# The order of the first sixteen weight chunks in a one-core hybrid decoder layer

## The chip, the core and the metric
The kernel runs on one core of a Trainium2 chip. The metric is the device time of one execution in microseconds (us). Before the change it is 1804.32 us, the median of three runs (1804.09 to 1804.88).

## The reference, cut to what matters
One decoder layer for 256 tokens of width 2048, in float32: a normed mixer with two parallel branches (mLSTM and RWKV-7), cross-attention into 256 memory tokens, and a gated feed-forward of width 8192. The change concerns its beginning:

```python
h = rms_norm(x, mix_pre_norm[l])          # x: 256 x 2048
proj = h @ w_in                           # 2048 x 10536
mlstm_p, rwkv_p, gate_p = split_cols(proj, (MLSTM_TOTAL, RWKV_TOTAL, GATE_TOTAL))
q, k, v, o, ir, fr = split_cols(mlstm_p, MLSTM_COLS)       # ir, fr: 4 columns each
r, kr, vr, wl, al, gl = split_cols(rp, RWKV_COLS)          # wl, al, gl: 64 + 64 + 160
```

The narrow outputs `ir`, `fr`, `wl`, `al`, `gl` together are 296 columns; `r` is 1024 columns wide. Everything after these projections is the same before and after the change.

## The kernel before, in words
A float32 product is built of three products of rounded numbers: each weight chunk and each tile of x is split into a high part (a rounded copy) and a low part (what the rounding left), and TensorE computes high x high, low x high and high x low. So for each chunk of weights ScalarE makes `wh` (L437) and VectorE makes `wl` (L463), and for each tile of x ScalarE makes the high part with the norm's gain in it and VectorE the low part (L68 is the helper through which these go; L191 is the one through which all matmuls go).

The work is a list of *blocks* (L1501 and on). A block has a list of weight chunks, a function that gives the tiles of x, and an evacuation that reads the sums. Block 0 holds the 296 narrow columns in 8 chunks `op`, each of which carries two k-tiles of x as well (552 KB: 128 partitions, 2 k-tiles, 256 + 296 columns). Block 1 holds 512 columns of `r` in 8 chunks of two k-tiles (`raw`, 512 KB). A chunk of block 1 needs the tiles of x that came with the narrow chunk of the same number.

`Feed` holds the order of chunks and runs ahead of the matmuls by numbers: `dma(n)` issues loads up to chunk n, `hi(n)` makes high parts, `lo(n)` low parts. While chunk i is multiplied, low parts are made up to i + 3 and loads are issued up to i + 7. There are four buffers for `raw` and five each for `wh` and `wl`. All loads but the first few are issued on SP's queue; ScalarE's queue takes three in the beginning (L405, L407, L412). The engines work in the order in which the program hands out instructions; there is no planner at run time.

The order before: `LEAD = 5` narrow chunks, then the other three in turn with the first chunks of block 1 (narrow 5, wide 0, narrow 6, wide 1, narrow 7), then wide 2 to 7 (L393, L594 to L602). The first two narrow chunks are treated apart (`first`, L441): piece by piece, chunk 0 on VectorE and ScalarE, chunk 1's high part on POOL. The wide chunk at place 6 is split in two pieces, so that its first k-tile is ready earlier (`pieces`, L427). `x_piece` (L624) splits the two k-tiles of x of one narrow chunk, and `pre_sm` and `pre_r0` say at which chunk that is done, and at which the squares of x are summed for the norm's statistics (`st0.add`).

Side work (evacuations and all that follows them) is cut into pieces by generators; `Spread.half` runs the next piece at each half of a chunk (each k-tile) if ScalarE and VectorE are thought to have room. The evacuation of block 0 is one such task (`sm_evac`, L672): it ends the statistics (`fold`, then a column of sums on TensorE, `var` on VectorE, a power on POOL, the matmuls `stb` on TensorE), scales the narrow outputs and transposes them. Before a new block starts, the evacuation of the block before the last must be through (`side.need`). Block 0's comes after its eighth chunk.

Of the kernel before, what the change touches and what calls it, by code (L numbers as in the profile page):

```python
# [22 lines left out]
DECAY = -math.exp(-0.5)  # L23
DFF = 8192
NSM = 296
LEAD = 5


_COLS = [
# [9 lines left out]
NPAR = _o  # L39
# [115 lines left out]
def _layer(ctx, tc, nc, d, dbg):  # L155
    act, dve = Meter(nc.scalar, 200.0, 0.83), Meter(nc.vector, 130.0, 1.04)
    pool, pe, sp = nc.gpsimd, nc.tensor, nc.sync
# [7 lines left out]
    def U(name, shape=None, dt=F32):  # L165
        return mp.tile(shape or [P, 8, S], dt, tag="U", bufs=7, name=name)

    def T2(name, shape=None, dt=F32):
        return mp.tile(shape or [P, 2, S], dt, tag="T2", bufs=6, name=name)

    def big(name, shape=None, dt=F32):
        return mp.tile(shape or [P, KD, S], dt, tag="big", bufs=2, name=name)
# [5 lines left out]
    def C(name, tag, shape=None, dt=F32):  # L178
        return mp.tile(shape or [P, S], dt, tag=tag, bufs=1, name=name)
# [7 lines left out]
    def aux(name, shape=None):  # L187
        return pp.tile(shape or [P, 512], F32, tag="aux", bufs=4, name=name)
# [4 lines left out]
    def keep_warm(n):  # L193

        q = aux("warm", [P, P])
        for _ in range(n):
            mm(q, ones.broadcast_to((P, P)), ones.broadcast_to((P, P)))


    par = cp.tile([P, NPAR], F32, name="par")  # L200
# [3 lines left out]
    def pcol(n, i=0, w=1):  # L204
        return par[:, PC[n] + i:PC[n] + i + w]
# [33 lines left out]
    def split(hi, lo, src):  # L239
        act.copy(hi, src)  # L240
        dve.tensor_sub(lo, src, hi)

    def split_gain(hi, lo, src, g):
        act.activation(hi, src, AF.Identity, scale=g)
        dve.scalar_tensor_tensor(lo, src, g, hi, op0=ALU.mult, op1=ALU.subtract)
# [37 lines left out]
    class Stat:  # L283


        def __init__(self, name, tag="ysb1", sq="au", home=None):
            self.name, self.tag, self.sq, self.home = name, tag, sq, home
            self.rc = cp.tile([P, 2], F32, name=name + "_c")
            self.n = 0
            self.done = False  # L290
# [99 lines left out]
    class Feed:  # L390
        def __init__(self):
            a, g = blocks[0]["srcs"], blocks[1]["srcs"]
            self.src = a[:LEAD] + [c for p in zip(a[LEAD:], g) for c in p] + g[len(a) - LEAD:]  # L393
            self.src += [s for b in blocks[2:] for s in b["srcs"]]
            self.raw, self.st, self.nd, self.ns, self.nl, self.nop = {}, {}, 0, 0, 0, 0

        def dma(self, upto):
            while self.nd <= min(upto, len(self.src) - 1):
                s = self.src[self.nd]
                if s.shape[-1] == NSM:  # L400
                    c = self.nop
                    self.nop += 1
                    r = op[c][:, :, S:]
                    if c == 0:
                        act.dma_start(ws0, d["w_s0"])  # L405
                        act.activation(mhalf[:, 0:1], mhalf[:, 0:1], AF.Copy)
                        act.dma_start(r[:, 1], s[:, 1])  # L407
                        for j in range(2):
                            sp.dma_start(xq[0][:, j], d["op"][0, :, j, 0:S])
                    elif c == 1:  # L410
                        sp.dma_start(op[1][:, 0], d["op"][1, :, 0])
                        act.dma_start(op[1][:, 1], d["op"][1, :, 1])  # L412
                    else:
                        sp.dma_start(op[c], d["op"][c])
                else:
                    r = wp.tile(list(s.shape), F32, tag="raw", bufs=4, name="raw")
                    sp.dma_start(r, s)
                self.raw[self.nd] = r
                self.nd += 1

# [5 lines left out]

        def pieces(self, n, *v):  # L427

            return [[t[:, k] for t in v] for k in range(2)] if n == LEAD + 1 else [v]

        def hi(self, upto):
            while self.ns <= min(upto, len(self.src) - 1):
                self.dma(self.ns)
                r = self.raw[self.ns]
                wh = self.staged("wh", r)
                for o, v in self.pieces(self.ns, wh, r):
                    nc.scalar.copy(o, v)  # L437
                self.st[self.ns] = [wh, None]
                self.ns += 1

        def first(self, c):  # L441

            r, wh, wl = self.raw.pop(c), self.staged("wh", self.src[c]), self.staged("wl", self.src[c])
            r = [ws0[:, 16:] if c == kj == 0 else r[:, kj] for kj in range(2)]
            if c == 0:
                nc.vector.tensor_copy(wh[:, 0], r[0])
            for kj in range(2):
                x_split(c, kj)
                if c:
                    pool.tensor_copy(wh[:, kj], r[kj])  # L450
                elif kj:
                    nc.scalar.copy(wh[:, kj], r[kj])
                nc.vector.tensor_sub(wl[:, kj], r[kj], wh[:, kj])
            self.st[c] = [wh, wl]
            self.ns = self.nl = c + 1

        def lo(self, upto):
            self.hi(upto)
# [15 lines left out]

    def run():
        feed = Feed()
        for c in range(8):
            x_load(c)
            feed.dma(c if c < LEAD else min(c * 2 - LEAD + 1, 10))
        i = 0  # L480
        pend = []

# [111 lines left out]
        side.ahead = lambda: feed.hi(feed.ns)  # L594
        side.ahead_lo = lambda: feed.lo(feed.nl)
        one, two = work(blocks[0]), work(blocks[1])
        for _ in range(LEAD):
            next(one)
        for _ in one:
            next(two)  # L600
        for _ in two:
            pass  # L602
        for b in blocks[2:]:
# [10 lines left out]
    op = [big("op0", [P, 3, 2, NX]), big("op1", [P, 3, 2, NX])]  # L614
    op = [op[c // 3][:, c % 3] for c in range(6)] + [U(f"op{c}", [P, 2, NX]) for c in (6, 7)]
    xq = [o[:, :, 0:S] for o in op]
    ws0 = C("ws0", "bg1", [P, 16 + NSM])
    xs0 = lambda k: (hh[:, k], hl[:, k])
    st0 = Stat("st0")

    def x_split(c, j):
        split_gain(hh[:, c * 2 + j], hl[:, c * 2 + j], xq[c][:, j], ws0[:, c * 2 + j:c * 2 + j + 1])

    def x_piece(c):  # L624
        for j in range(2):
            x_split(c, j)

    def x_load(c):
        if c == 6:
            sp.dma_start(par[:, 16:NPAR], d["par"][:, 16:NPAR])  # L630

    def pre_sm(ci, feed):
        if ci == 0:
            keep_warm(7)
            for c in range(2):
                feed.first(c)
            x_piece(2)
            feed.lo(2)
        if ci < 3:
            x_piece(ci + 3)  # L640
        if ci == 4:
            x_piece(6)
            sp.dma_start(con, d["con"])
        for c in {3: (0,), 5: (1,), 6: (2, 3), 7: (6,)}.get(ci, ()):
            st0.add(xq[c])

    def pre_r0(ci, feed):
        if ci == 0:
            x_piece(7)
        if ci == 1:  # L650
            st0.add(xq[4])
            st0.add(xq[5])
        if ci == 3:
            sp.dma_start(up[0:64], d["w_up"])
        if ci == 4:
            sp.dma_start(up[64:128], d["a_up"])
# [15 lines left out]
    def sm_evac(ps):  # L672
        dve.tensor_scalar(om, pcol("mu", 0, 27), -1.0, 1.0, op0=ALU.mult, op1=ALU.add)
        dve.tensor_scalar(oka, pcol("ka", 0, 8), -1.0, 1.0, op0=ALU.mult, op1=ALU.add)
        st0.add(xq[7])
        yield from st0.finish(4, 2)
        zs = C("zs", "bg1", [P, 2, NSM])
        for t in range(2):
            act.activation(zs[:, t], ps[t], AF.Copy, scale=st0.rc[:, t:t + 1])
        yield  # L680
        yield
        q = [aux("smT", [P, 2, S]) for _ in range(3)]
        for (o, j), c, n in (((0, 0), 0, P), ((0, 1), P, P), ((1, 0), 256, 32), ((1, 1), 288, 4), ((2, 0), 292, 4)):
            for t in range(2):
                pe.transpose(q[o][0:n, j, t * P:(t + 1) * P], zs[:, t, c:c + n], ident)
        wa, gl = C("wa", "m0"), T2("gl")
        gl0, gl1 = gl[:, 0], gl[:, 1]
        shiftmix(wa, q[0][:, 0], 24)
        shiftmix(gl0, q[0][:, 1], 25)
        yield  # L690
        shiftmix(gl1, q[1][:, 0], 26, slice(0, 32))
        R = [T2("rows") for _ in range(4)]
        M["rows"] = R
        tasks["gates"] = side.add(gates(), chain=1)
        act.copy(R[0][0:4, 0], q[1][0:4, 1])
        act.copy(R[0][0:4, 1], q[2][0:4, 0])
        act.activation(wa[0:64], wa[0:64], AF.Tanh)
        tasks["smr"] = side.add(sm_rest(wa, gl0, gl1), back=True)
        yield
# [1321 lines left out]
```

## Time and profile before

| what | value |
| --- | --- |
| median of 3 runs | 1804.32 us |
| profiled execution | 1804.55 us |
| its span, first to last instruction | 1802.7 us |
| TensorE busy | 1793.1 us, 99% of the span |
| VectorE busy | 1325.1 us, 74% |
| ScalarE busy | 1056.8 us, 59% |
| POOL busy | 28.7 us, 2% |
| moved by DMA | 351.61 MB, mean 195 GB/s |

The profiled execution is one run; its span lies 1.85 us inside its time. The shares are means over the whole kernel, and the change is in its first 45 us, so the rows further down are of that stretch for the most part. In the names, PE is TensorE, DVE VectorE, ACT ScalarE, POOL GpSimd, SP the engine that issues most DMAs; a "q" behind a name is the engine's sequencer. `tm` are the sums of block 0 in the opening, `fm` those of block 1; `hx` the tiles of x.

### The profile page before, as it was taken

The numbers are of one execution on the slowest core, as the hardware profiler recorded it, in microseconds if no ns is written. First come the engines' busy times: TensorE is split into PE (matmuls) and PEld (weight loads), VectorE is DVE, ScalarE is ACT, GpSimd is POOL, SyncE is SP. The second block draws the span as 40 slices with busy tenths as digits, with TensorE's granted clock in tenths as the row PEclk, the third lists the DMA queues.
The fourth block names the chain that finished last, engine by engine and source line by source line (L and its number), as shares of the span: only waits on it lengthen the run. The fifth ranks groups of instructions, "written<-read, shape, count | busy, mean of one in ns | idle before, by whom it ended". The sixth has DMA issues, their size and how long they took to land.

```text
span 1802.7 us, 30168 instructions
## 1 busy us (share of the span) xinstructions
PE 1793.1 (99%) x11814; PEld 1636.5 (91%) x11814; DVE 1325.1 (74%) x1948; ACT 1056.8 (59%) x1642; POOL 28.7 (2%) x51
## 2 busy tenths in 40 slices
PE   9999999999999999999999999999999999999998
PEld 8999988888888999899999999999999988888887
DVE  7869995765765768789877788777777775666665
ACT  7576454654554665676666666665565564455454
POOL 0100000100100000000000000000000000000000
PEclk9999999999999999999999999999999999999999
DMA  8656564354556775556666666666666666666664
GB/s 282 206 170 187 164 188 151 120 177 154 188 190 207 246 233 176 187 170 189 210 199 201 208 195 204 209 194 201 207 195 200 205 203 218 208 204 207 201 200 151
DMA packets 99135, 351.61 MB, mean 195 GB/s; under 512 B 10896, under 2 KB 13968, under 8 KB 98864
## 3 DMA queue, kind: packets, MB, share of 16 engines
q1 hardware_dynamic: 97888, 347.38, 60.4%
q8 instruction: 93, 1.52, 0.3%
q0 software_dynamic: 384, 1.18, 0.3%
q10 hardware_dynamic: 720, 1.12, 0.2%
q14 instruction: 50, 0.41, 0.1%
HBM read 347.01 MB, written 2.10 MB: 194 GB/s over the span
## 4 chain that ended last, share of the span: by engine, by line
PE 99%; DVE 0%; DMA 0%; ACT 0%; issue 0%; SPq 0%; DVEq 0%; ACTq 0%
PE fm L191 55%; PE tm L191 39%; PE gram L191 0%; PE Y L191 0%; PE lv L191 0%; DMA op<-in_op_dram 0%; PE X L191 0%; PE num L191 0%; PE zwa L191 0%; PE U L191 0%; PE gramA L191 0%; PE xo L191 0%; PE zg L191 0%; PE Tn L191 0%; PE mT L1353 0%; PE st L191 0%
## 5 line engine op out<-in xcount | busy, mean ns | idle before, releaser
L463 DVE TENSOR_TENSOR wl<-raw,wh 128x1024 fp32r<-128x1024 f32 (+1 forms) x641 | 767.9, 1219 | 145.8 <-ACT wh L437 143.4
L437 ACT CAST wh<-raw 128x1024 fp32r<-128x1024 f32 (+1 forms) x641 | 656.0, 1044 | 109.7 <-PE tm L191 60.7
L191 PE MATMUL fm<-fx,wh 128*128 128x512 f32 (+1 forms) x2240 | 672.8, 364 | 0.6 <-DVE fx L68 0.4
L191 PE MATMUL fm<-fx,wl 128*128 128x256 f32 x2048 | 558.3, 273 | 0.0
L191 PEld LDWEIGHTS fm<-fx,wh 128*128 128x128 f32 x2240 | 409.2, 190 | 49.8 <-DVE fx L68 1.0
L191 PEld LDWEIGHTS fm<-fx,wl 128*128 128x128 f32 x2048 | 393.2, 192 | 0.0
L191 PE MATMUL tm<-wh,as 128*128 128x512 f32 x1024 | 304.6, 379 | 0.0
L191 PE MATMUL tm<-wh,hx 128*128 128x512 f32 (+1 forms) x832 | 243.9, 378 | 1.8 <-ACT hx L68 1.5
L191 PEld LDWEIGHTS tm<-wh,as 128*128 128x128 f32 x1024 | 193.5, 189 | 27.4
L191 PE MATMUL tm<-wl,as 128*128 128x512 f32 x512 | 194.0, 379 | 0.0
L68 ACT COPY ul<-fm 128x256 f32<-128x256 f32 x128 | 44.9, 373 | 225.1 <-PE fm L191 225.1
L191 PE MATMUL fm<-hx,wh 128*128 128x256 f32 x1024 | 174.5, 277 | 0.0
L191 PEld LDWEIGHTS tm<-wh,hx 128*128 128x128 f32 x832 | 151.0, 189 | 22.5 <-POOL wh L450 1.7
L191 PEld LDWEIGHTS fm<-hx,wh 128*128 128x128 f32 x1024 | 155.4, 192 | 1.1
L191 PE MATMUL tm<-wl,hx 128*128 128x512 f32 (+1 forms) x416 | 152.5, 373 | 0.1
L68 DVE TENSOR_TENSOR us<-fm,ul 128x256 f32<-128x256 f32 x128 | 48.5, 421 | 130.9 <-ACT ul L68 130.9
L191 PE MATMUL fm<-hx,wl 128*128 128x256 f32 x512 | 140.8, 275 | 0.0
L68 ACT CAST as<-ac 128x256 fp32r<-128x256 f32 x128 | 45.6, 405 | 153.0 <-PE tm L191 153.0
L68 DVE TENSOR_TENSOR as<-ac,as 128x256 fp32r<-128x256 f32 x128 | 48.6, 422 | 91.3 <-ACT as L68 91.3
L191 PEld LDWEIGHTS tm<-wl,as 128*128 128x128 f32 x512 | 96.8, 189 | 13.7
L191 PEld LDWEIGHTS fm<-hx,wl 128*128 128x128 f32 x512 | 98.3, 192 | 0.0
L191 PEld LDWEIGHTS tm<-wl,hx 128*128 128x128 f32 x416 | 77.5, 189 | 10.7 <-DVE wl L463 0.3
(374 smaller groups left out, 1883.8 us busy)
## 6 DMA issues: line engine op xcount, KB each, us to landing
raw<-in_w_fw_dram SPq DMA_DIRECT2D x232, 512.0 KB, 4.2
raw<-in_w_in_dram SPq DMA_DIRECT2D x160, 512.0 KB, 3.7
raw<-in_w_fd_dram SPq DMA_DIRECT2D x128, 512.0 KB, 4.0
raw<-in_w_br_dram SPq DMA_DIRECT2D x32, 512.0 KB, 4.3
raw<-in_w_mw_dram SPq DMA_DIRECT2D x24, 512.0 KB, 4.6
raw<-in_w_fu_dram SPq DMA_DIRECT2D x24, 512.0 KB, 4.0
raw<-in_w_mo_dram SPq DMA_DIRECT2D x8, 512.0 KB, 4.2
raw<-in_w_xk_dram SPq DMA_DIRECT2D x8, 512.0 KB, 4.3
```

Of the source, the lines that this page charges most:

```text
L68: return f(out, *a, **k)
L191: pe.matmul(out, lhsT, rhs, start=start, stop=stop, skip_group_check=True)
L437: nc.scalar.copy(o, v)
L463: nc.vector.tensor_sub(o, v, h)
```

## The change
The first sixteen chunks come in another order: narrow 0, wide 0, narrow 1, wide 1, narrow 2, wide 2, then narrow 3 to 7, then wide 3 to 7. The wide chunk at place 1 is loaded in four quarters (k-tile by column half), two on SP's queue and two on ScalarE's. Narrow chunk 1 is loaded whole on SP's queue, and its high part is made on ScalarE in one instruction as for the later ones; only narrow chunk 0 is still treated apart. The split of a narrow chunk's x now stands in `hi`, just before the chunk's own high part, in place of the places written out by hand. The squares for the statistics are summed at other chunks, those of chunks 6 and 7 in the evacuation. `par` is loaded after the ninth chunk.

```diff
-LEAD = 5
+PAIRS = 3
...
-            self.src = a[:LEAD] + [c for p in zip(a[LEAD:], g) for c in p] + g[len(a) - LEAD:]
+            self.src = [c for p in zip(a[:PAIRS], g) for c in p] + a[PAIRS:] + g[PAIRS:]
...
-                    elif c == 1:
-                        sp.dma_start(op[1][:, 0], d["op"][1, :, 0])
-                        act.dma_start(op[1][:, 1], d["op"][1, :, 1])
                     else:
                         sp.dma_start(op[c], d["op"][c])
                 else:
                     r = wp.tile(list(s.shape), F32, tag="raw", bufs=4, name="raw")
-                    sp.dma_start(r, s)
+                    if self.nd == 1:
+                        for kj in range(2):
+                            for e, q in ((sp, slice(0, 256)), (act, slice(256, 512))):
+                                e.dma_start(r[:, kj, q], s[:, kj, q])
+                    else:
+                        sp.dma_start(r, s)
...
-            return [[t[:, k] for t in v] for k in range(2)] if n == LEAD + 1 else [v]
+            return [[t[:, k] for t in v] for k in range(2)] if n == 1 else [v]
...
                 self.dma(self.ns)
+                if self.ns in self.xc:
+                    x_piece(self.xc[self.ns])
...
-        def first(self, c):
+        def first(self):
...
-                if c:
-                    pool.tensor_copy(wh[:, kj], r[kj])
-                elif kj:
-                    nc.scalar.copy(wh[:, kj], r[kj])
+                if kj:
+                    nc.scalar.copy(wh[:, 1], r[1])
...
-        for c in range(8):
-            x_load(c)
-            feed.dma(c if c < LEAD else min(c * 2 - LEAD + 1, 10))
+        feed.dma(8)
+        sp.dma_start(par[:, 16:NPAR], d["par"][:, 16:NPAR])
+        feed.dma(11)
...
-        for _ in range(LEAD):
+        for _ in range(PAIRS):
             next(one)
+            next(two)
         for _ in one:
-            next(two)
+            pass
...
+    def adds(ci, when):
+        for c in when.get(ci, ()):
+            st0.add(xq[c])
...
     def pre_sm(ci, feed):
         if ci == 0:
             keep_warm(7)
-            for c in range(2):
-                feed.first(c)
-            x_piece(2)
-            feed.lo(2)
-        if ci < 3:
-            x_piece(ci + 3)
+            feed.first()
         if ci == 4:
-            x_piece(6)
             sp.dma_start(con, d["con"])
-        for c in {3: (0,), 5: (1,), 6: (2, 3), 7: (6,)}.get(ci, ()):
-            st0.add(xq[c])
+        adds(ci, {4: (2,), 5: (3,), 6: (4,), 7: (5,)})
...
     def pre_r0(ci, feed):
-        if ci == 0:
-            x_piece(7)
-        if ci == 1:
-            st0.add(xq[4])
-            st0.add(xq[5])
+        adds(ci, {1: (0,), 2: (1,)})
...
     def sm_evac(ps):
...
+        st0.add(xq[6])
         st0.add(xq[7])
```

## Rows read from the trace of the kernel before

**Rows 1.** The page's chain of what ended last: shares by engine.
```profile
PE 99%; DVE 0%; DMA 0%; ACT 0%; issue 0%; SPq 0%; DVEq 0%; ACTq 0%
```

**Rows 2.** TensorE's waits, whole span: total us, times, longest us.
```profile
PE tm L191 <- ACT hx L68: 1.5, 1, 1.5
...
PE fm L191 <- DVE fx L68: 0.4, 1, 0.4
PE X L191 <- DVE so L68: 0.3, 1, 0.3
PE xo L191 <- ACT xv L68: 0.2, 1, 0.2
```

**Rows 3.** Windows of 4 us: busy us by engine, clock, DMA share, GB/s.
```profile
4.00:8.00 4.00, 2.43 (x14) 1.72 (x13) 1.81 (x6) 1.69 (x5) 0.59 (x2) 1.00 0.98 337
...
12.00:16.00 4.00, 4.00 (x34) 4.00 (x34) 3.87 (x8) 4.00 (x9) 0.00 (x0) 1.00 1.03 414
```

**Rows 4.** The chain in order of time, 0 to 60: start, us, what.
```profile
17.02 2.68 PE fm L191 x24
19.70 1.51 PE tm L191 x12
...
33.89 0.04 issue
33.93 0.71 PE stb L191 x4
```

**Rows 5.** Timeline, all engines, 4 to 16: start, us, what [idle before <-releaser].
```profile
4.34 1.04 PE L191 MATMUL tm<-wh,hx 128*128 128x296 f32 x4
...
6.10 0.43 PE L191 MATMUL tm<-wl,hx 128*128 128x296 f32 x2
...
7.38 0.93 ACT L68 ACTIVATE hx<-op,ws 128x256 fp32r<-128x256 f32 x2 [2.31 <-DMA op<-in_op_dram]
...
8.84 0.91 ACT L68 ACTIVATE hx<-op,ws 128x256 fp32r<-128x256 f32 x2 [0.53 <-DMA op<-in_op_dram]
...
12.33 0.67 PE L191 MATMUL tm<-wh,hx 128*128 128x296 f32 x4
...
15.09 1.13 ACT L437 CAST wh<-raw 128x512 fp32r<-128x512 f32 x2
```

**Rows 6.** Timeline of SP's issues, 3 to 12.
```profile
3.78 0.33 SPq L414 DMA_DIRECT2D op<-in_op_dram  x1
...
10.25 0.36 SPq L417 DMA_DIRECT2D raw<-in_w_in_dram  x1
11.77 0.33 SPq L643 DMA_DIRECT2D con<-in_con_dram  x1
```

**Rows 7.** DMAs begun at 1.25, 1.66, 4.15, 24.37, 28.64: KB, us to landing.
```profile
op<-in_op_dram ACTq DMA_DIRECT2D x1, 148.0 KB, 3.2
...
op<-in_op_dram ACTq DMA_DIRECT2D x1, 276.0 KB, 6.1
...
op<-in_op_dram SPq DMA_DIRECT2D x1, 552.0 KB, 9.0
...
raw<-in_w_in_dram SPq DMA_DIRECT2D x1, 512.0 KB, 3.5
...
raw<-in_w_in_dram SPq DMA_DIRECT2D x1, 512.0 KB, 4.6
```

**Rows 8.** Timeline of VectorE, 7 to 33.
```profile
7.92 0.62 DVE L68 SCALAR_TENSOR_TENSOR hx<-op,ws,hx 128x256 fp32r<-128x256 f32 x1 [1.96 <-ACT hx L68]
...
9.61 0.87 DVE L68 SCALAR_TENSOR_TENSOR hx<-op,ws,hx 128x256 fp32r<-128x256 f32 x2
...
11.09 0.87 DVE L68 SCALAR_TENSOR_TENSOR hx<-op,ws,hx 128x256 fp32r<-128x256 f32 x2
...
15.73 1.29 DVE L463 TENSOR_TENSOR wl<-raw,wh 128x512 fp32r<-128x512 f32 x2
...
32.02 0.15 DVE L68 TENSOR_SCALAR var<-st 128x2 f32<-128x2 f32 x1
```

More of the change, by code (lines that the diff above doesn't have):

```diff
@@ L392, in __init__ @@
             a, g = blocks[0]["srcs"], blocks[1]["srcs"]
-            self.src = a[:LEAD] + [c for p in zip(a[LEAD:], g) for c in p] + g[len(a) - LEAD:]
+            self.src = [c for p in zip(a[:PAIRS], g) for c in p] + a[PAIRS:] + g[PAIRS:]
             self.src += [s for b in blocks[2:] for s in b["srcs"]]
-            self.raw, self.st, self.nd, self.ns, self.nl, self.nop = {}, {}, 0, 0, 0, 0
+            self.raw, self.st, self.nd, self.ns, self.nl, self.xc = {}, {}, 0, 0, 0, {}
         def dma(self, upto):
@@ L400, in dma @@
                 if s.shape[-1] == NSM:
-                    c = self.nop
-                    self.nop += 1
+                    c = self.xc[self.nd] = len(self.xc)
                     r = op[c][:, :, S:]
@@ L439, in hi @@
                 self.ns += 1
-        def first(self, c):
[L443 to L446, printed above, removed]
-            for kj in range(2):
-                x_split(c, kj)
-                if c:
-                    pool.tensor_copy(wh[:, kj], r[kj])
-                elif kj:
-                    nc.scalar.copy(wh[:, kj], r[kj])
+        def first(self):
+            r, wh, wl = self.raw.pop(0), self.staged("wh", self.src[0]), self.staged("wl", self.src[0])
+            r = [ws0[:, 16:], r[:, 1]]
+            nc.vector.tensor_copy(wh[:, 0], r[0])
+            for kj in range(2):
+                x_split(0, kj)
+                if kj:
+                    nc.scalar.copy(wh[:, 1], r[1])
                 nc.vector.tensor_sub(wl[:, kj], r[kj], wh[:, kj])
-            self.st[c] = [wh, wl]
-            self.ns = self.nl = c + 1
+            self.st[0] = [wh, wl]
+            self.ns = self.nl = 1
         def lo(self, upto):
@@ L626, in x_piece @@
             x_split(c, j)
-    def x_load(c):
-        if c == 6:
-            sp.dma_start(par[:, 16:NPAR], d["par"][:, 16:NPAR])
+    def adds(ci, when):
+        for c in when.get(ci, ()):
+            st0.add(xq[c])
     def pre_sm(ci, feed):
```

## The prediction
> **What bounds the kernel now.** I read the page's chain of what ended last first [rows 1]: 99% of it is TensorE. With TensorE's work unchanged, the time can move only where TensorE stands still. Its table of waits names the places inside the work [rows 2]: 1.5 us before a `tm` matmul, which is in the opening, and 0.9 us in three places of the middle. The windows show the opening filling up [rows 3]: from 4 to 8 us TensorE is busy for 2.43 of 4, from 12 to 16 for all of it, with VectorE at 3.87, ScalarE at 4.00 and the DMA engines full. The granted clock is 1.00 in both, so no clock term arises.
>
> I write N0 to N7 for the narrow chunks (552 KB each, with two k-tiles of x; 12 matmuls of 296 columns) and W0 to W7 for the 512-column chunks (512 KB; 24 matmuls of 256 columns). At full rate N costs TensorE 1.51 us and W 2.68 us [rows 4].
>
> The opening in order of time [rows 5]: N0 runs from 4.34 to 6.53. Then N1 is awaited; ScalarE's split of its x starts at 7.38, after 2.31 us of idling on the DMA. N2's split starts at 8.84, again on the DMA: that is its landing. TensorE is through with N2 and starts N3 at 12.33. From there it stands next at 33.89, for 0.04 us [rows 4]. Three N, 4.53 us of work, would at full rate have ended at 4.34 + 4.53 = 8.87; they end at 12.33. The opening loses 3.46 us, and no more can be won there.
>
> **The change part by part.**
> *Order.* TensorE's third item stays a narrow chunk, but the second is now W0 and not N1. N1 takes N2's place: third to be used, third to land. If N1 lands at L, the row of N2 says when TensorE is through with it: 12.33 - 8.84 = 3.49 us after. By then it has done 2 x 1.51 + 2.68 = 5.70 us of work where it had done 4.53. The gain is 5.70 - 4.53 = 1.17 us, less (L - 8.84).
>
> *When N1 lands.* Later N chunks land every 1.4 to 1.5 us: N2 by 8.84, and SP's issue at 10.25 waited for the landing of N3, the next at 11.77 for that of N4 [rows 5, 6]. Ahead of N1 there are now 512 KB (W0) where there were 552 (N1 ahead of N2): 40 KB less at 552 KB per 1.41 us is 0.10 us, so L = 8.74. Against that, N1 is issued later: eight DMAs are begun before it where N2 had six before it, and the ninth issue began at 3.78 in the kernel before [rows 6]. An issue at 24.4 with little else in flight landed 3.5 us later [rows 7]; 3.78 + 3.5 = 7.3 comes before 8.74, so the data ahead hide the later issue. Bounds: half a chunk's time (0.7) earlier, 8.0, to a whole one (1.4) later, 10.1. I take 8.74, the nearest to the row: 1.17 + 0.10 = 1.27 us.
>
> *W0 in quarters.* Its first k-tile takes a ScalarE copy (1.13 for two, near 0.6 each), a VectorE subtraction (1.29 for two, near 0.68) [rows 5, 8] and, estimated from the 0.03 to 0.06 between an engine's end and the next one's start in these rows, 0.15 of hand-overs: 1.45 us from landing to TensorE's third matmul. 22 matmuls of 0.112 (2.68 / 24) follow, 2.46 us; together 3.9. N1 loses nothing while W0 ends by 12.23 - 1.51 = 10.7, that is while its first two quarters land by 6.8. N0's last part landed at 1.25 + 3.2 = 4.45 [rows 7]; half of 512 KB at the steady rate would be in at 5.1; N1's first half, the nearest row, came just before 7.38, say 7.35. I take 6.2, between them: W0 ends near 10.1, hidden. At 7.35 it ends at 11.25, N1 at 12.76, and the gain is 5.70 - 4.53 - 0.43 = 0.74. The second k-tile has until about 7.3, since the first keeps TensorE busy for 1.34. ScalarE issues two of the quarters while it is idle; should one wait for a landing there, N0's split waits with it for the 0.4 us of an issue, which TensorE's wait for W0 covers.
>
> The Trainium skill, "DMA: Bandwidth & Descriptors", section "Issuing engines are not separate DMA queues", speaks against the quarters: DMAs started by the scalar and the sync engine run on the same 16 DMA engines and interleave, so a second issuer saves only time of issue. The trace agrees: N1's two halves on two queues took from 4.45 to 7.76 (1.66 + 6.1), 3.3 us for 552 KB, against 1.41 for a whole chunk later [rows 5 to 7]. Were W0 in at that steady rate (4.45 + 1.31 = 5.76), the gain would be 1.27; by the row of the halves it is 0.74.
>
> *The run of five narrow chunks.* VectorE takes 1.48 us for an N (9.61 to 11.09 [rows 8]), near 1.2 for a W (1.29 for W0's two halves, which overlap a little with what follows) and, estimated from the same rate of elements, 0.65 for an added square; TensorE 1.51 and 2.68. Counting on from N1's first split at 9.3, with 0.4 for waits on ScalarE in the first pair, VectorE is done with N1 at 11.0, W1 12.4, N2 13.9, W2 15.1, N3 16.6, N4 18.1, N5 20.2, N6 21.7, N7 23.8, W3 25.6 (a square before N5, N7 and W3 each). TensorE, through N1 at 12.2, comes to W1 there, to N3 at 19.1, N7 at 25.1, W3 at 26.6. The lead shrinks from 2.5 to 1.0 us, and W1 is tied (0.05 us charged). POOL's two casts for N1 go; ScalarE's copy that replaces them is part of the pattern of N2.
>
> *What is late next.* At the end of the statistics VectorE's `var` (32.02) is followed by a power on POOL and TensorE's `stb` matmuls (33.93) [rows 4, 8], already tied with TensorE. That chain moves one W later with the end of the narrow block: TensorE is due at 33.93 + 2.68 - g for a gain g. VectorE ran from 7.92 to 32.02, 24.1 us; now it starts with N1's split at 9.3, has W0 (1.2) behind it and W7 (1.2) added, so `var` starts at 33.4 and `stb` can run 1.91 later, at 35.3. At g = 1.2 TensorE is due at 35.4: 0.1 us of cover. The chain caps the gain at about 1.3, unless N1 lands earlier, which moves both.
>
> *Sum.* 1.27 - 0.05 = 1.2 us. The profiled execution took 1804.55 (span 1802.7 and 1.85 around it), 0.23 over the median of 1804.32. 1803.35 by the first, 1803.1 by the median, which I forecast.
>
> **The rivals.**
> 1. *W0 lands like N1 did.* For: that row is the only one of a transfer in this place on two queues. Gain 0.74, time 1803.6.
> 2. *Better than that.* The DMA engines moved 337 KB per us from 4 to 8 us and 414 from 12 to 16 [rows 3]. If less of the first is lost, L falls to 8.0: gain 1.9, 1802.4. The ceiling of 3.46 gives 1800.9. Against: `stb`.
> 3. *Slower: TensorE stands before `stb`.* `var` is queued on VectorE behind the subtraction of W7. W7's transfer needs the buffer that W3's subtraction frees, at 25.6, because five narrow chunks now come before W3. With the 4.6 us of an issue at 28.7 [rows 7] and about 1.1 of copy, W7 is ready at 31.3, before its turn at 32.2. With the longest landing seen, 9.0, it is ready at 35.7: 3.5 late, 0.1 of cover, 3.4 lost and 1.2 won, 1806.5. It decides from 1.3 us of lateness. Against: little else is in flight then.
> 4. *Given back later.* The evacuation of the narrow block, and all that hangs on it, comes two half-steps later against the matmuls. The three stalls of the middle [rows 2] may go, or as many come anew: up to 0.9 either way, 1802.2 to 1804.0. No row says which.
>
> **How the numbers follow.** Forecast, gains of 0.6 to 1.9: 0.52. Rival 1, or 4 taking a part (gain 0 to 0.6): 0.22. Rival 2: 0.12. Rival 3 and other losses: 0.14, most within 1 us. The range 1801.3 to 1805.0 leaves out the top of rival 2 (0.03) and half of the losses (0.07). A measurement of this kernel tells about 0.2%, 3.6 us, from no change. The ceiling of 3.46 lies inside that, so faster than 1800.7 needs luck in the middle as well: 0.03. Slower than 1807.9 is beyond rival 3's bound: 0.04 for what no row shows. Same: 0.93.
>
> **What would show it.** In the changed profile: W0's first matmul between 6.6 and 7.5; N1's split on ScalarE at 8.6 to 8.9; TensorE through N1 near 12.2 and without a stall from there to `stb`; `var` near 33.4 and `stb` near 35.4. It is wrong if W0's first quarters land after 6.8, N1 after 9.9, or if TensorE waits over 0.3 us before `stb` or for VectorE between N5 and W3.

## The result and the profile after

The changed kernel takes 1808.41 us (median of 16 runs, 1806.66 to 1810.16) against 1804.30 (16 runs of the kernel before, 1803.89 to 1804.88): 4.1 us longer, ratio 1.0023 with a 95% interval of 1.0016 to 1.0031. The forecast was 1803.1, the range 1801.3 to 1805.0. It was wrong in sign. Its profiled execution took 1807.99 us with a span of 1805.8, 3.1 us more than before; outside the span lie 2.19 us where it was 1.85.

The waits of TensorE come first again. The columns are as in [rows 2].

```profile
PE fm L191 <- ACT wh L440: 2.4, 1, 2.4
...
PE tm L191 <- DVE wl L463: 0.6, 1, 0.6
```

Of the 1.5 us of [rows 2] 0.3 are left, and two new waits stand at the top: 2.4 us of an `fm` matmul for ScalarE's `wh`, and 0.6 of a `tm` matmul for VectorE's `wl`. The chain of the changed kernel, in order of time from 0 to 45, says where the first comes from (start, us, what):

```profile
0.74 2.87 DMA ws<-in_w_s_dram
3.61 0.02 issue
3.63 6.64 DMA raw<-in_w_in_dram
10.28 0.02 issue
10.30 0.63 ACT wh L440
10.93 0.04 issue
10.97 3.23 PE fm L191 x12
14.20 1.63 PE tm L191 x12
15.83 2.68 PE fm L191 x24
...
22.70 7.55 PE tm L191 x60
30.25 5.36 PE fm L191 x48
35.61 0.34 PE st L191 x4
...
38.74 0.45 PE stb L191 x4
```

A DMA is issued at 3.63, right after the landing of `ws` at 3.61, and lands at 10.28. The issues and landings show which one it is; first the timeline of ScalarE and its queue in the changed kernel, then loads begun at 1.65 to 1.66, 2.59, 3.44 and 3.63 with KB and us to landing:

```profile
3.63 0.33 ACTq L416 DMA_DIRECT2D raw<-in_w_in_dram  x1
...
10.30 0.62 ACT L440 CAST wh<-raw 128x512 fp32r<-128x512 f32 x1 [3.86 <-DMA raw<-in_w_in_dram]
10.82 0.91 ACT L68 ACTIVATE hx<-op,ws 128x256 fp32r<-128x256 f32 x2
```
```profile
raw<-in_w_in_dram SPq DMA_DIRECT2D x1, 128.0 KB, 3.5
raw<-in_w_in_dram ACTq DMA_DIRECT2D x1, 128.0 KB, 4.1
...
op<-in_op_dram SPq DMA_DIRECT2D x1, 552.0 KB, 5.2
...
raw<-in_w_in_dram SPq DMA_DIRECT2D x1, 512.0 KB, 6.2
raw<-in_w_in_dram ACTq DMA_DIRECT2D x1, 128.0 KB, 6.6
```

It is the fourth quarter of W0. The second had been issued on the same queue at 1.66. This one was held until `ws` had landed, while SP issued N1 at 2.59 and W1 at 3.44; it landed behind both. The trace names the *landing signal* of each load, the semaphore that tells that its data are there: the first eight loads have eight different ones, this ninth has that of `ws`, the first, once more, and W1, the tenth, that of x's first half. In the text of the kernel the quarter stands eighth and N1 ninth; what gave them the signals in the other order was not traced. W0's first k-tile was there at 5.76 (1.66 + 4.1), and TensorE had done it by 8.6; then it stood for 2.4 us. N1, in at 7.8 (2.59 + 5.2), could not fill the gap: ScalarE's split of its x stood behind the copy of the held quarter and began at 10.82.

The stall brought a second loss. Windows of the changed kernel, columns as in [rows 3]:

```profile
8.60:11.00 2.40, 0.03 (x1) 0.03 (x1) 0.05 (x1) 0.70 (x2) 0.00 (x0) 0.98 1.04 420
...
12.00:13.00 1.00, 1.00 (x6) 1.00 (x6) 1.00 (x3) 1.00 (x2) 0.00 (x0) 0.50 1.01 415
...
14.60:16.00 1.40, 1.40 (x13) 1.40 (x13) 1.40 (x4) 1.40 (x3) 0.00 (x0) 1.00 1.01 387
```

After the stall the granted clock is 0.50 (1.2 GHz) from 10.9 to 14.3, and 12 matmuls of W0's second k-tile take 3.23 us where 1.34 is the full rate [rows 4].

The second new wait is far behind the opening. Timelines of ScalarE, the changed kernel first, then the kernel before at the same work:

```profile
259.11 2.13 ACT L68 COPY Lt<-L 128x512 f32<-128x512 f32 x2 [7.15 <-DVE tmp L68]
261.14 1.04 ACT L440 CAST wh<-raw 128x1024 fp32r<-128x1024 f32 x1
```
```profile
252.69 1.11 ACT L68 COPY Lt<-L 128x512 f32<-128x512 f32 x1 [7.72 <-DVE tmp L68]
253.71 1.04 ACT L437 CAST wh<-raw 128x1024 fp32r<-128x1024 f32 x1
254.66 1.13 ACT L68 COPY Lt<-L 128x512 f32<-128x512 f32 x1
```

Two copies of side work now stand back to back in front of a weight copy that used to lie between them; its low part comes late, and TensorE stands for 0.56 us at 262.9. Counting the `fm` and `tm` matmuls through in both traces, the changed kernel is 1.85 us behind from 208 to 256 us and 2.8 from 268 to the end: this place costs 1.0 us.

### The profile page after: what moved, and what is told of

Same layout as the page of the kernel before. It is cut to its first block, busy times and chain, and to the rows that moved or that the text cites. A ratio compares the mean times of both kernels' runs of the same rounds, so it can differ in the third digit from the quotient of the medians.

```text
span 1805.8 us, 30166 instructions
## 1 busy us (share of the span) xinstructions
PE 1794.3 (99%) x11814; PEld 1637.6 (91%) x11814; DVE 1324.0 (73%) x1947; ACT 1056.9 (59%) x1643; POOL 27.5 (2%) x49
## 4 chain that ended last, share of the span: by engine, by line
PE 98%; DVE 1%; DMA 1%; ACT 0%; issue 0%; DVEq 0%; ACTq 0%
PE fm L191 55%; PE tm L191 38%; PE gram L191 0%; PE Y L191 0%; DMA raw<-in_w_in_dram 0%; DVE wl L463 0%; PE lv L191 0%; PE X L191 0%; PE num L191 0%; PE zwa L191 0%; PE U L191 0%; PE gramA L191 0%; PE xo L191 0%; PE zg L191 0%; PE Tn L191 0%; PE mT L1344 0%
```

## The experiments

The theory after this reading (A): a load held for a landing signal costs the stall and, through it, the clock. (D): the evacuation's later place costs the 1.0 us near 260. The rivals were that ScalarE's queue is starved behind SP's large loads whenever its loads are issued (B), and that the run of five narrow chunks costs the time (C). Each run has a median of 11; the difference is to the kernel before on the same chip, whose medians were 1804.22 to 1804.39. An interval reaches some 1.6 us to either side, so what is said below of smaller differences rests on the waits in the traces and not on the medians alone.

| kernel | median us | to before | ratio, 95% interval |
| --- | --- | --- | --- |
| x_one_load | 1805.12 | +0.8 | 0.9994 to 1.0012 |
| three_pieces | 1804.46 | +0.1 | 0.9994 to 1.0011 |
| whole_w0 | 1804.88 | +0.5 | 0.9995 to 1.0012 |
| fill | 1806.60 | +2.3 | 1.0003 to 1.0021 |
| fill10 | 1806.74 | +2.4 | 1.0005 to 1.0023 |
| lead4 | 1806.42 | +2.1 | 1.0002 to 1.0020 |
| x_one_pairs2 | 1804.69 | +0.4 | 0.9993 to 1.0011 |
| x_one_rest15 | 1803.28 | -1.0 | 0.9987 to 1.0005 |
| after_rest15 | 1807.02 | +2.6 | 1.0005 to 1.0022 |
| three_rest15 | 1803.31 | -1.1 | 0.9985 to 1.0003 |
| four_on_sp_rest15 | 1805.75 | +1.4 | 0.9997 to 1.0014 |
| four_on_sp_x_one | 1804.88 | +0.7 | 0.9995 to 1.0013 |
| old_split | 1804.39 | 0.0 | 0.9991 to 1.0009 |
| old_split3 | 1806.83 | +2.6 | 1.0005 to 1.0023 |

**No load held on ScalarE's queue.** x_one_load, three_pieces and whole_w0 each take loads away, in three ways, from the changed kernel:

```diff
-                        for j in range(2):
-                            sp.dma_start(xq[0][:, j], d["op"][0, :, j, 0:S])
+                        sp.dma_start(xq[0], d["op"][0, :, :, 0:S])            # x_one_load
...
-                        for kj in range(2):
-                            for e, q in ((sp, slice(0, 256)), (act, slice(256, 512))):
-                                e.dma_start(r[:, kj, q], s[:, kj, q])
+                        for e, q in ((sp, slice(0, 256)), (act, slice(256, 512))):
+                            e.dma_start(r[:, 0, q], s[:, 0, q])
+                        sp.dma_start(r[:, 1], s[:, 1])                        # three_pieces
...
+                        sp.dma_start(r, s)                                    # whole_w0
```

> The two loads of x in the first narrow chunk become one, so that only eight loads are begun before the second narrow chunk is through; all else as in the changed kernel. Theory A (the fourth quarter of W0 is the ninth load and is held on ScalarE's queue until the landing signal of ws comes free; that late issue costs a stall of 2.4 us and then 1.7 us at the half clock): the fourth quarter is issued by 2.6 instead of 3.63 and lands by 7, TensorE has no stall over 0.5 us between 6.5 and 11, the clock stays at 1.00, N1 lands near 8.1, and the time is 1802.4 to 1803.2. Rival B (data of ScalarE's queue are starved behind SP's large loads, whenever they are issued): the quarter lands after 9 again, time 1807.5 to 1808.5. Rival C (the stall is covered anyway and the run of five narrow chunks costs the time): no stall in the opening, yet VectorE is late between N5 and W3, time 1806 or more.

> W0's second k-tile is loaded whole on SP's queue, its first k-tile in two halves on the two queues as in the changed kernel: one load less, and none on ScalarE that must wait. Theory A: as with x in one load, no stall, 1802.4 to 1803.2. Rival B (starving on ScalarE's queue): the one quarter left there landed at 5.74 before, so B gives the same here. Rival C: 1806 or more.

> W0 is loaded whole by one load on SP's queue. Theory A: the quarters are worth little, since W0 may land as late as 6.8 unnoticed: W0 lands at 5.8 to 6.5, no wait of the signals, time 1802.4 to 1803.4, equal to the three pieces within 0.5 us. Rival (the quarters bring the first k-tile so much earlier that they earn their issue): W0 whole lands near 7.5, time 0.7 us or more above the three pieces.

The waits of TensorE with x in one load, the fourth quarter (KB, us to landing), and the windows of the opening:

```profile
PE tm L191 <- ACT hx L68: 1.2, 1, 1.2
...
PE tm L191 <- DVE wl L462: 0.6, 1, 0.6
```
```profile
raw<-in_w_in_dram ACTq DMA_DIRECT2D x1, 128.0 KB, 5.3
```
```profile
4.00:8.00 4.00, 2.79 (x18) 2.19 (x17) 2.23 (x5) 2.22 (x5) 0.00 (x0) 1.00 1.03 356
8.00:12.00 4.00, 4.00 (x36) 4.00 (x35) 3.54 (x6) 3.63 (x8) 0.00 (x0) 1.00 1.02 412
```

The fourth quarter, still on ScalarE's queue but issued at 2.18, lands 5.3 us later, at 7.5; the 2.4 us are gone, TensorE is busy for all of 8 to 12, the clock stays. So B and C fall. (The 1.2 us are the wait for all of N0's x in one load.) All three kernels come back to the time before and no further: 1.3 to 1.9 us above the slowest that A alone had led me to expect. The quarters themselves matter little: a whole load is 0.4 us behind three pieces, though it came at 6.9, later than the 5.8 to 6.5 expected, and TensorE waited 1.0 us for it. In all three, TensorE's 0.56 near 260 is still there.

**The clock.** The stall stays, but matmuls on ones are put into it.

```diff
+                    if i == 1 and kj == 0:
+                        keep_warm(5)          # fill; 11 in fill10
```

> The changed kernel with 5 more warm-up calls (10 matmuls on ones, 2.4 us) put between the two k-tiles of W0, where TensorE stands still; nothing else. Theory A1 (of the loss, the half clock after the stall is 1.7 us): the clock stays at 1.00, W0's second k-tile takes 1.6 us instead of 3.2, N1 1.51 instead of 1.63 and more, and the time falls to 1806.4 to 1807.0. Rival A2 (the clock costs nothing here, since VectorE and the landings set the pace of W0's second half and of N1): the clock stays at 1.00 but the time stays within 0.4 us of 1808.4.

> As the five calls between W0's k-tiles, but eleven: at the full clock ten matmuls on ones took 1.1 us, so five calls covered less than half of the stall and the clock still fell in the profiled run. Theory A1 (the half clock after the stall costs 1.6 to 1.9 us): granted clock 1.00 from 4 to 40 us, W0's second k-tile in 1.6 us, time 1806.3 to 1806.8. Rival A2: clock 1.00 and time 1808 and more.

Windows of fill10:

```profile
8.00:12.00 4.00, 3.96 (x34) 3.72 (x33) 0.55 (x1) 1.20 (x3) 0.00 (x0) 1.00 1.03 407
12.00:16.00 4.00, 3.80 (x32) 3.81 (x33) 3.84 (x8) 4.00 (x8) 0.00 (x0) 1.00 1.03 416
```

With eleven calls TensorE is never idle for long, the clock stays at 1.00, and the median is 1.7 us under the changed kernel's although no useful work begins earlier (the calls even hold W0's second k-tile back by 0.5 us, to 11.47): A1. The two profiled executions are only 0.8 us apart, with the matmuls after N1 starting at 14.93 against 15.67, so the size of 1.7 rests on the medians. Five calls last only 1.1 us at the full clock; in the profiled run the clock fell all the same (mean clock 0.998, 1808.42 us), while the other ten runs, at 0.999 to 1.0, took 1805.8 to 1807.3; the median is 1806.60.

**The evacuation's later place.** lead4 is the kernel before with `LEAD = 4`; x_one_pairs2 is x_one_load with `PAIRS = 2`; in the third, a count in the background task that the evacuation starts is changed:

```diff
-        for _ in range(17):
+        for _ in range(15):
             yield
```

> The kernel before with LEAD = 4: its old opening, in which W0, W1 and W2 come one place earlier, so that the narrow block ends after three wide chunks instead of two, and its evacuation comes two half-steps later against the matmuls, as in the changed kernel. Theory D (with x in one load, TensorE's lead over the kernel before falls from 1.94 to 0.82 us near 260 us, 0.56 of it idle; that is the evacuation's later place, not the opening): the same idle of about 0.56 us before a tm matmul appears near 262, and the time is 1805.1 to 1805.7. Rival (that loss comes of the new opening, for instance of TensorE being ahead of its weights): nothing new near 262, time 1804.0 to 1804.6.

> x of the first chunk in one load, and two pairs instead of three: N0 W0 N1 W1, then N2 to N7, then W2 to W7. The narrow block ends after two wide chunks, as in the kernel before. Theory D: the idle near 260 us is gone, the gain of the opening (1.7 to 1.9) stays, unless VectorE falls behind in a run of six narrow chunks, which would show before W2; time 1802.6 to 1803.4. Rival of D: the idle near 260 is still there, 1804.0 to 1805.2.

> x of the first chunk in one load, three pairs, and the task that follows the narrow block's evacuation in the background waits 15 instead of 17 half-steps before it begins, so that it stands where it stood before the change. If the idle near 260 us comes of this task's place: it is gone, 1803.6 to 1804.2. If it comes of another follower of the evacuation (the gates, or the order of the bulk tasks): it stays, and the time is that of x in one load, 1804.3 to 1805.2.

TensorE in lead4 near 262:

```profile
262.66 0.48 PE L191 MATMUL tm<-wl,hx 128*128 128x512 f32 x1 [0.56 <-DVE wl L463]
```

The same idle comes with the old opening as soon as the narrow block ends one wide chunk later, and it is absent with two pairs and with 15 half-steps. So D holds, and the follower is `sm_rest`. Of lead4's 2.1 us, its own opening loses 0.84 (in the count of matmuls, from 208 to 256 us) and the place near 260 another 1.2. x_one_pairs2 lost its gain to another wait, 0.66 us before `stb`: with six narrow chunks in a row the statistics' chain comes too late. Which link leads from `sm_rest` to the copies at 259 was not traced. The later place also costs something outside the span: time less span is 2.0 to 2.2 us in the medians of all kernels with the later evacuation and 17 half-steps, lead4 among them, and 1.8 in the others and before. Why is not shown.

**Both together.** The 15 half-steps in the changed kernel, and with W0 in three pieces.

> The changed kernel with 15 instead of 17 waiting half-steps in the background task and nothing else: the held quarter of W0 stays. Theory (two separate losses that add: the held load with the clock it drops, 3.3 to 4.1 us, and the background task's place, 1.1 us): the opening is unchanged (a stall of about 2.4 us, the half clock after it), the idle of 0.56 near 263 us is gone, time 1807.0 to 1807.5. Rival (the background task matters only if the opening is early): 1808.0 to 1808.7.

> W0 in three pieces (second k-tile whole on SP) and the 15 half-steps. If the two losses were all that hid the forecast gain, the opening gains 1.0 to 1.9 and nothing is lost near 260: 1802.8 to 1803.5, as with x in one load. If one load for x was itself of use: 0.5 us or more above that kernel's 1803.28.

| | 17 half-steps | 15 half-steps |
| --- | --- | --- |
| fourth quarter held | +4.1 (changed kernel) | +2.6 |
| none held (three pieces) | +0.1 | -1.1 |

To within the noise the losses add: the held load costs 3.7 to 4.0 us and the background task's place 1.2 to 1.5. What remains is 1.1 us under the kernel before, near the forecast's 1.2; its interval still reaches no change. It has the lowest profiled span of all, 1801.5. Its chain in order of time:

```profile
8.12 2.72 PE fm L191 x22
10.84 1.51 PE tm L191 x12
12.35 2.68 PE fm L191 x24
...
32.13 0.34 PE st L191 x4
32.47 2.79 PE fm L191 x24
35.26 0.45 PE stb L191 x4
```

**Is it the hold, or the time of issue?** All quarters on SP, so that N1 is the ninth load; the same with x in one load, so that N1 is the eighth and is not held; and cuts of N1's second half in the kernel before.

```diff
-                            for e, q in ((sp, slice(0, 256)), (act, slice(256, 512))):
+                            for e, q in ((sp, slice(0, 256)), (sp, slice(256, 512))):   # four_on_sp_*
...
-                        act.dma_start(op[1][:, 1], d["op"][1, :, 1])
+                        for q in (slice(0, 192), slice(192, 384), slice(384, NX)):
+                            act.dma_start(op[1][:, 1, q], d["op"][1, :, 1, q])          # old_split3
```

> All four quarters of W0 on SP's queue and the 15 half-steps: the ninth load is now N1, on SP, and it is N1 that waits for the landing of ws. Theory A (what costs is not that a load waits, but that W0's quarter is begun after N1 and W1 and lands behind them): the four quarters land by 7, N1 is issued near 3.6 and still lands by 9.2, no stall over 0.6 us, clock 1.00, time 1802.8 to 1804.0. Rival (any load held for a signal in the opening costs 2 us or more): 1806 or more.

> All four quarters of W0 on SP, 15 half-steps, and x of the first chunk in one load, so that N1 is the eighth load and is not held. Theory A (the hold itself costs, on either queue): N1 is issued by 3.1, lands by 8.6 instead of 9.98, the 2.0 us stall before N1 and the half clock are gone, time 1802.8 to 1803.8. Rival (four small loads in a row on SP's queue delay N1 by their own overhead): N1 lands near 10 again, 1805 to 1806.

> The kernel before, its order untouched, but the second half of N1 on ScalarE's queue cut into two loads (columns 0 to 275 and the rest), so that nine loads are begun before the fifth narrow chunk and the last of ScalarE's is held for a landing. Theory A: that piece is issued at 3.6 or later, lands after N2 (8.8), TensorE's wait before N1's second k-tile grows by 1 to 2 us, and the time rises by 1 to 3 us, to 1805.3 to 1807.3, more if the clock falls. Rival (the late issue hurts only together with the new order): the piece lands by 8 and the time stays at 1804.3.

> The kernel before with the second half of N1 in three loads on ScalarE's queue instead of one, so that the last of them is the ninth or tenth load and is held. Theory A: that piece is issued at 3.6 or later and lands after 9.5, TensorE's wait before N1's second k-tile grows by 1 us or more, time 1805.3 to 1807.5. Rival (a held load costs only in the new order): 1804.2 to 1804.8 although the piece is held. If no load of N1 is held, the run tells nothing of this.

N1 in four_on_sp_rest15, then in four_on_sp_x_one (its issue, KB and us to landing), then TensorE in old_split3:

```profile
3.73 0.33 SPq L410 DMA_DIRECT2D op<-in_op_dram  x1
...
op<-in_op_dram SPq DMA_DIRECT2D x1, 552.0 KB, 6.3
```
```profile
3.52 0.46 SPq L409 DMA_DIRECT2D op<-in_op_dram  x1
...
op<-in_op_dram SPq DMA_DIRECT2D x1, 552.0 KB, 7.2
```
```profile
11.20 0.77 PE L191 MATMUL tm<-wh,hx 128*128 128x296 f32 x4 [1.79 <-POOL wh L451]
```

With all quarters on SP, N1 is held until 3.73 and lands at 10.0; TensorE stands for 2.0 us and the clock falls after it. My expectation that only a load behind others suffers fell. Without the hold N1 still lands at 10.7, because SP's own issues, about 0.5 us each, bring it to 3.52; in x_one_load, with the same quarters on two queues, it was issued at 2.56 and landed at 8.4. So the hold is one way, and a queue of small loads another, to issue a load late; what costs is the late issue. In the traces of all these kernels the ninth load has the landing signal of one of the first two again, on whichever queue it is. In the old order, cutting N1's half in two held no load of N1 and changed nothing; cut in three, its last piece was held to 3.83 and landed 6.8 us later, TensorE stood for 1.79 us before N1's second k-tile, and the time rose by 2.6 us, with the clock at 1.00 throughout the opening. The new order is not needed for it.

## Why the prediction was wrong, point by point

*W0 in quarters: the step that failed.* It said that, should one of ScalarE's quarters wait for a landing, N0's split would wait with it for the 0.4 us of an issue, which TensorE's wait for W0 covers. That much came true: N0's split began at 4.01, behind the held issue, and TensorE waited 0.3 us for it. But it priced the hold as time of the engine, not as lateness of the data. The load that was held landed 6.6 us after its issue, at 10.28, against the 7.3 allowed in the same paragraph for the second k-tile, and TensorE stood for 2.4 us. The working had a hold at 3.78 for the ninth load and gave it to N1, ninth in the kernel's text; in the run the quarter had the ninth signal. None of the signs of being wrong named the second half of W0: its first half and N1 landed in time.

*When N1 lands.* The bound for a late issue, 3.78 + 3.5 = 7.3, was taken from a lone transfer at 24.4 [rows 7], though the load begun at 4.15 in the same rows took 9.0. In the opening, loads issued at 3.52 to 3.83 took 6.3 to 7.2 us. The estimate 8.74 itself was near: 8.5 in three_rest15 (its split at 8.50), 7.8 in the changed kernel, where a quarter that should have been ahead of N1 came behind it.

*No clock term.* True of the kernel before, and carried over without asking what a new stall would do: 1.7 us by the medians.

*Order.* Right. In three_rest15 TensorE is through N1 at 12.35 (forecast 12.2), having done a wide chunk in place of a narrow one.

*The run of five narrow chunks.* Right: 60 `tm` matmuls in 7.55 us, five times 1.51, in the changed kernel too.

*What is late next.* Right: `stb` at 35.26 in three_rest15, forecast 35.4, without a wait; `var` came at 32.82, forecast 33.4.

*Given back later, rival 4.* The mechanism was named, the size bounded by the stalls then there (0.9); it is 1.0 in the profile and 1.2 to 1.5 in the medians, which hold the part outside the span too, and it was treated as even odds when it could only be judged by what follows the evacuation.

In sum, by the medians: 1.1 won where no load is held, 3.7 lost by the held load, 1.5 by the background task: +4.1.

## What to carry to other kernels

When a change adds loads to an opening, count the loads in the order in which they get their landing signals (here not the order of the text), mark the first that must wait for a landing, and price it by when its data come, behind everything issued meanwhile. Cutting a load into more pieces spends issues and landing signals that the next load needs. And a block that ends one chunk later takes its whole train of background work along: look at each count of half-steps that was set for the old place.

## What the runs showed of the hardware that was not expected

A load of 552 KB issued at 2.59 in the opening landed after 5.2 us, one issued at 3.52 to 3.73 after 6.3 to 7.2, though 24.4 us into the kernel before 512 KB took 3.5 [rows 7]. In four_on_sp_rest15 the DMA engines moved 182 KB per us from 5.5 to 7.0 and 247 from 7.0 to 8.5, against 361 in three_rest15:

```profile
5.50:7.00 1.50, 1.50 (x12) 1.50 (x12) 1.32 (x4) 1.02 (x2) 0.00 (x0) 1.00 0.93 182
7.00:8.50 1.50, 1.50 (x16) 1.50 (x15) 0.47 (x1) 0.00 (x0) 0.00 (x0) 1.00 0.63 247
```

Why such a load takes so long there is open; a late issue alone does not lower the rate, for in the changed kernel it is 341 KB per us from 4 to 8, against 242 in four_on_sp_rest15.

The clock did not answer to the length of the idle time alone. TensorE stood for 2.0 us before N1 in four_on_sp_rest15 and for 2.3 us in four_on_sp_x_one; the windows from 12 to 16 of the first and then of the second:

```profile
12.00:16.00 4.00, 3.96 (x20) 3.74 (x19) 3.83 (x6) 3.79 (x8) 0.00 (x0) 0.59 1.02 418
```
```profile
12.00:16.00 4.00, 3.70 (x27) 3.38 (x28) 3.74 (x7) 3.83 (x7) 0.00 (x0) 1.00 1.02 418
```

After the shorter idle the clock fell, after the longer it did not; the second kernel's median is 0.9 us less. One kernel may do both: in four_on_sp_rest15 seven runs had a mean clock of 0.998 and took 1805.7 to 1806.3 us, the other four had 0.999 and took 1804.2 to 1804.9, as if the clock fell in the seven alone. That may be part of why the changed order varies more from run to run (1806.7 to 1810.2 against 1803.9 to 1804.9 before); the rest of it is open.
